# Wider streams and zero-padded rows in the small products of a decoder's mixers

## The chip, the cores and the metric

The kernel runs on one core of a Trainium2 chip. The metric is the device time of one execution in microseconds. Each kernel is run several times; the median counts. The kernel before took 3079.33 us (median of three runs, 3071.02 to 3081.82).

## What is computed

A decoder trunk of two layers over 512 tokens, with 16 learned meta tokens put ahead of them and dropped at the end; the width is 1024. Cut to what matters:

```python
h = concatenate([meta, x])                                   # 528 x 1024
for l in range(2):
    h = layer_norm(ALPHA * h + 0.5 * swiglu(h, ffn1...))     # width 2816
    h = layer_norm(ALPHA * h + mixer(h, ...))
    h = layer_norm(ALPHA * h + 0.5 * swiglu(h, ffn2...))
return h[16:]

def mixer(x):
    z = x @ w_in                       # convolution branch, RWKV branch, two gates
    yc = conv_branch(glu_a, glu_b)     # 31 taps per channel, norm, product
    yr = rwkv_branch(zr)               # per head of 64, step by step over the tokens:
                                       #   S = S * w_t + (S @ -kk_t) (kk_t a_t)^T + v_t k_t^T
                                       #   y_t = S @ r_t
    return (sigmoid(gate_c) * yc + sigmoid(gate_r) * yr) @ w_out
```

In the RWKV branch `kk` is divided by its norm over the 64 columns of its head. All values are float32.

## The kernel before

Activations lie with the channels on the 128 partitions and the tokens along the row. A wide product of float32 values is made of three products of a split format: each operand is split into a high and a low part, and high*high, high*low and low*high are added up in PSUM. The weights stream through all the time: load from HBM on SP's queue, high part on ScalarE, low part on VectorE or by an adding transfer that GpSimd issues.

A layer is FFN, mixer, FFN. In the trace the two mixers with their input projections lie at about 400 to 1040 and 1935 to 2565 us. In a mixer the 16 heads are worked in four groups of four, `q` = 0 to 3, each with two pairs of heads (two heads fill 128 partitions). For each group:

- `prep` projects r, k and v (products of L246), and scales them. The norms of `kk` come from L1144: the squares (128 channels by 128 tokens as weights) are multiplied by every fourth column of a block matrix of ones, 32 columns, of which two are read: one of each head. Five such products make a pair's norms; each shows as two instructions in the trace, as all plain float32 products do (the split ones show as one).
- `scores` multiplies within each chunk of 64 tokens (L1250 transposes, L1259), and within the 16 meta tokens (L1236). The scores of the meta tokens, the keys, the values and some results lie in the tile `small`, 16 partitions by 2048.
- `substitution` (VectorE) inverts 16 by 16 blocks; `inverse` joins them to inverses of 64 by 64: one product of 64 columns (L1333), then three rounds of `x = dt + vt^T x` (L1340). The first round makes all 64 columns; the second and third only the columns 32 to 63, as the first 32 are right after one round.
- `meta` works off the meta tokens before the scan begins: scores times values (L1365), the small inverse times that (L1371), then the state that the scan starts from and, in the first layer, the meta tokens' own output (both by the helper `pairs`, L1459). All contract over the 16 meta tokens, so they use 16 of the 128 rows of the array.
- `scan` walks over the eight chunks: state product (L1415), a copy on ScalarE, two sets of four products (L1428 and L1431), a copy on ScalarE, products with the scores (L1436), and the new state `sv` on VectorE, which the next chunk's L1415 waits for.

Between these stand the projections of the next group, of the convolution's input and of the gates, all products of L246, as fill. VectorE also does the convolution's taps (L1088). The program is written as an interleaving of generators with tables of numbers, and a scheduler, which has prices of its own for each instruction, then sets the order of each engine's queue by priorities. Each engine works its queue in order. Some idle places are filled with products whose results are never read (`keep`, L227).

Of the kernel before, what the change touches and what calls it, by code (L numbers as in the profile page):

```python
# [7 lines left out]
F32 = mybir.dt.float32  # L8
# [8 lines left out]
P = 128  # L17
# [3 lines left out]
NM = 16  # L21
# [8 lines left out]
HS = 64  # L30
# [68 lines left out]
class Trunk:  # L99
# [868 lines left out]
    def mixer_begin(self, zs, filler):  # L968

        nc, mp, d = self.nc, self.mp, self.d
        z = self.tmp()
        self.token_mix(zs[0], 24, z)
        nc.scalar.activation(z[0:64, :], z[0:64, :], AF.Tanh)
        x = self.tmp("kp", 1, F32R), self.tmp("k2", 1, F32R)
        self.split(z, *x)
        z = self.tmp()
        self.token_mix(zs[1], 25, z)
        nc.scalar.activation(z, z, AF.Tanh, scale=0.5)  # L980
        xg = self.tmp("a", 1, F32R), self.tmp("pinv", 1, F32R)
        nc.scalar.activation(xg[0], z, AF.Copy, bias=1.0)
        nc.vector.scalar_tensor_tensor(xg[1], z, 1.0, xg[0].bitcast(F32), op0=ALU.add,
                                       op1=ALU.subtract)
        filler(START[0])
        acts = (lambda o: (AF.Sigmoid, self.v1("w0", o), 1.0),
                lambda o: (AF.Tanh, self.half[:, 0, o:o + 1], 0.5))
        up = [(d["w_up"], slice(0, 64)), (d["a_up"], slice(64, P))]

        room = mp.tile([P, 4, KT, P], F32R, name="sb", bufs=1)  # L990
        w = self.wunit(*((r, u[self.l].rearrange("r (o c) -> r o c", c=P)) for u, r in up),
                       dst=[room[:, 0], room[:, 1]])

        self.bi = 0
        stage = {}

        def lowrank(w, x, o, r, dst, act=None):
            if act is None:
                t = self.tmp("v", 4) if o % 2 else mp.tile([P, NCH * 4, 32], F32, name="b4",
                                                           bufs=B4)  # L1000
                t = t if o % 2 else t.rearrange("p a b -> p (a b)")[:, 0:T]
            else:
                if o == 0:
                    stage[r.start] = self.rows().rearrange("p q e f t -> p (q e f) t")
                t = stage[r.start][:, o]
            both = self.sc() if self.bi % 2 == 0 else None
            self.bi += 1
            for h in range(2):
                s = slice(h * (T // 2), (h + 1) * (T // 2))
                pm = (self.sm(("tr", "ch")[h]) if both is None else both[:, h])[:, :T // 2]  # L1010
                for j, (a, b) in enumerate(((0, 0), (0, 1), (1, 0))):
                    nc.tensor.matmul(pm, w[a][r, o, :], x[b][r, s], start=j == 0, stop=j == 2)
                to = t[:, s]
                if both is not None:
                    if h == 0:
                        continue
                    pm, to = self.pv(both), self.tv(t)
                if act is None:
                    nc.vector.tensor_scalar_mul(to, pm, 0.5)
                else:  # L1020
                    f, b, scale = act(o)
                    nc.scalar.activation(to, pm, f, bias=b, scale=scale)
            nc.sync.dma_start(out=dst[o * P:(o + 1) * P, :], in_=t)

        wg = self.wunit(d["g_up"][self.l].rearrange("r (o c) -> r o c", c=P),
                        dst=[room[:, 2], room[:, 3]])
        todo = [[lambda o=o, r=r, act=act, dst=dst: lowrank(w, x, o, r, dst, act)
                 for o in range(KT)]
                for (_, r), act, dst in zip(up, acts, (self.ds, self.as_))]
        todo.append([lambda o=o: lowrank(wg, xg, o, slice(0, P), self.ggs) for o in range(KT)])  # L1030
        for i, (j, o) in enumerate(LOW):
            todo[j][o]()
            if i % LOWSTEP == LOWSTEP - 1:
                filler(1)
            self.taps(TAP0[0])
        filler(START[1])
        self.sb = mp.tile([P, NCH, 4, 2 * C], F32, name="sb", bufs=1)

        self.ut = mp.tile([P, NCH * 2, C], F32, name="ut")

        small = mp.tile([NM, 2048], F32, name="small")
        self.small, o = {}, 0
        for name, n in (("kb", 512), ("s", 256), ("v", 256), ("u", 256), ("y0", 256), ("y1", 256), ("y2", 256)):
            self.small[name] = small[:, o:o + n]
            o += n

        self.dd = mp.tile([P, NCH * 2, 2, C], F32, name="dd")
        nc.gpsimd.memset(self.dd, 0.0)
# [66 lines left out]
    def prep_pair(self, q, p, Q):  # L1115
        nc, mp = self.nc, self.mp
        pc = Q["pc"]
        i = 2 * q + p
        cs = slice(i * P, (i + 1) * P)
# [5 lines left out]
        nk, r = G[:, 1, 0, :], G[:, 1, 1, :]  # L1125
        kp = self.tmp("kp", 1)
        self.token_mix(self.proj(16 + 8 + i), 8 + i, kp)
        sq = self.tmp()
# [3 lines left out]
        a = self.tmp("a", 1)  # L1132
# [5 lines left out]

        pn = self.sc()
        pn, p0 = pn[:, 0], pn[:, 1]  # L1140
        tr = p0[:, NM:NM + 160]
        for j in range(5):
            k0 = NM + j * P if j < 4 else 0
            nc.tensor.matmul(tr[:, 32 * j:32 * j + 32], sq[:, k0:k0 + P], self.bones[:, ::4],  # L1144
                             start=True, stop=True)
        tr = tr[:, ::16]
        rs = mp.tile([P, 10], F32, name="rs", bufs=1)
        rx = self.tmp()[:, :4 * P].rearrange("p (j h v) -> p j h v", j=4, h=2)
        rx0 = mp.tile([P, P], F32, name="rx", bufs=1)[0:NM].rearrange("a (h v) -> a h v", h=2)
# [54 lines left out]
        for h in range(2):  # L1204
            nc.tensor.matmul(pn[:, h, :T // 2], rk, k2[:, h * (T // 2):(h + 1) * (T // 2)],
                             start=True, stop=True)
# [7 lines left out]
    def scores(self, q, Q):  # L1214


        nc, mp = self.nc, self.mp
        G, FB, SB = Q["G"], Q["FB"], self.sb
        tr = self.sm("tr")
        for p in range(2):  # L1220
# [1 line left out]
                nc.tensor.transpose(tr[0:NM, f * 256 + p * P:f * 256 + (p + 1) * P],  # L1222
                                    FB[p][:, f * NM:(f + 1) * NM], self.ident)
        kb0 = self.small["kb"]
        nc.scalar.copy(kb0, tr[0:NM, :])
        Q["kb0"] = kb0.rearrange("p (f h v) -> p f h v", f=2, h=4)
        ps = self.sc()
        ps = [ps[:, 0], ps[:, 1]]
        s0 = Q["s0"] = self.small["s"].rearrange(
            "a (e p f g t) -> a e p f g t", e=2, p=2, f=2, g=2)  # L1230
        for e in range(2):
            p0 = ps[e][0:NM, 0:4 * 2 * NM].rearrange("a (p f x) -> a p f x", p=2, f=2)
            r = slice(HS * e, HS * e + HS)
            for p in range(2):
                for f in range(2):
                    nc.tensor.matmul(p0[:, p, f, :], FB[p][r, f * NM:(f + 1) * NM],  # L1236
                                     G[r, p, 1, :, 0:NM], start=True, stop=True)
            nc.vector.tensor_tensor(s0[:, e].rearrange("a p f g t -> a (p f) g t"),
                                    ps[e][0:NM, 0:4 * 2 * NM]
                                    .rearrange("a (x g t) -> a x g t", g=2, t=NM),  # L1240
                                    self.msk0[:, None].to_broadcast([NM, 4, 2, NM]), op=ALU.mult)
            nc.sync.dma_start(out=self.ms0[q, e::2].rearrange("h j t -> j h t"),
                              in_=s0[:, e, :, 1, 0, :])
        yield
        for c in range(NCH):
            cs = slice(NM + c * C, NM + (c + 1) * C)
            fs = slice(2 * cs.start, 2 * cs.stop)
            ps = self.sc()
# [7 lines left out]
            for p in range(2):  # L1256
                for e in range(2):
                    r = slice(HS * e, HS * e + HS)
# [58 lines left out]
    def inverse(self, q, g, Q):  # L1317
# [3 lines left out]
        nc, mp = self.nc, self.mp  # L1321
# [13 lines left out]
        x = dt  # L1335
        for c0 in (0, 2 * NM, 2 * NM):
            cs = slice(c0, C)
            for i in range(N):
                for r in halves:
                    nc.tensor.matmul(ps[r, i, cs], vt[r, i], x[r, i, cs], start=True, stop=True)  # L1340
            nc.vector.tensor_tensor(y[:, :, cs], ps[:, :, cs], dt[:, :, cs], op=ALU.add)
            x = y
        out = Q["G"].rearrange("a p e f t -> a (p e) f t")
# [9 lines left out]
    def meta(self, q, Q):  # L1353
# [3 lines left out]
        tr = self.sm("tr")  # L1357
        for p in range(2):
            nc.tensor.transpose(tr[0:NM, p * P:(p + 1) * P], Q["v"][p][:, 0:NM], self.ident)
        v0 = hc(self.small["v"])  # L1360
        nc.scalar.copy(v0, hc(tr[0:NM, 0:256]))
        s0, kb0 = Q["s0"], Q["kb0"]
        ch = self.sm("ch")
        for h in range(4):
            nc.tensor.matmul(ch[0:NM, h * HS:(h + 1) * HS], s0[:, h % 2, h // 2, 0, 0, :],  # L1365
                             v0[:, h, :], start=True, stop=True)
        sa0 = hc(self.small["u"])
        nc.scalar.copy(sa0, hc(ch[0:NM, 0:256]))
        ch = self.sm("ch")
        for h in range(4):  # L1370
            nc.tensor.matmul(ch[0:NM, h * HS:(h + 1) * HS], xt0[:, h, :], sa0[:, h, :],  # L1371
                             start=True, stop=True)
        nc.scalar.copy(sa0, hc(ch[0:NM, 0:256]))
        ch = self.sm("ch")
        self.pairs([(ch[HS:P, h * HS:(h + 1) * HS], kb0[:, 0, h, :], v0[:, h, :],
                     kb0[:, 1, h, :], sa0[:, h, :]) for h in range(4)])
# [4 lines left out]
        if not self.last:  # L1381
            ch = self.sm("ch")
            self.pairs([(ch[0:NM, h * HS:(h + 1) * HS], s0[:, h % 2, h // 2, 0, 1, :], v0[:, h, :],
                         s0[:, h % 2, h // 2, 1, 1, :], sa0[:, h, :]) for h in range(4)])
            y0 = self.small[f"y{q % 3}"].rearrange("a (m h v) -> a m h v", m=1, h=4)
            nc.scalar.copy(y0[:, 0], hc(ch[0:NM, 0:256]))
            Q["y0"] = y0

    def scan(self, q, Q):

# [378 lines left out]
```

## Time and profile before

| | |
|---|---|
| median of three runs | 3079.33 us |
| profiled execution, its own time | 3072.55 us |
| its span from the first to the last instruction | 3070.8 us |
| TensorE busy | 2996.3 us |
| VectorE busy | 2276.7 us |
| ScalarE busy | 1439.3 us |
| GpSimd busy | 178.3 us |
| mean granted clock of TensorE | 0.982 |

TensorE's busy time counts a product from its start until its modelled end, so what one costs in a stream is read from the starts of neighbouring groups, not from its duration. The page's clock row gives, for 40 slices of the span, the share of TensorE's full clock that was granted; a table by stretches gives it for any stretch.

### The profile page before, as it was taken

The numbers are of one execution on the slowest core, as the hardware profiler recorded it, in microseconds if no ns is written. First come the engines' busy times: TensorE is split into PE (matmuls) and PEld (weight loads), VectorE is DVE, ScalarE is ACT, GpSimd is POOL, SyncE is SP. The second block draws the span as 40 slices with busy tenths as digits, with TensorE's granted clock in tenths as the row PEclk, the third lists the DMA queues.
The fourth block names the chain that finished last, engine by engine and source line by source line (L and its number), as shares of the span: only waits on it lengthen the run. The fifth ranks groups of instructions, "written<-read, shape, count | busy, mean of one in ns | idle before, by whom it ended". The sixth has DMA issues, their size and how long they took to land. (4 is left out here: it accounts for less than half of the span.)

```text
span 3070.8 us, 64144 instructions
## 1 busy us (share of the span) xinstructions
PE 2996.3 (98%) x26076; PEld 2875.1 (94%) x26076; DVE 2276.7 (74%) x4689; ACT 1439.3 (47%) x2553; POOL 178.3 (6%) x286
## 2 busy tenths in 40 slices
PE   9999999999999999999999999999999999999998
PEld 9999989889888899999999999998889889999998
DVE  5766777788876768676776768778988748677767
ACT  4544464344455535444444444543454545254443
POOL 0110000000000000000001100000000000001100
PEclk9999999899999999999999999999999989999999
DMA  7665444335465554565545654443354645556652
GB/s 197 145 145 130 117 141 144 88 82 130 106 148 139 164 150 124 133 154 124 128 128 141 142 136 112 153 134 97 86 141 105 150 118 175 148 124 148 151 139 62
DMA packets 556149, 405.29 MB, mean 132 GB/s; under 512 B 89306, under 2 KB 500798, under 8 KB 555854
## 3 DMA queue, kind: packets, MB, share of 16 engines
q1 hardware_dynamic: 520302, 308.49, 35.2%
q0 software_dynamic: 30944, 84.18, 14.9%
q10 hardware_dynamic: 4608, 8.52, 0.7%
q8 instruction: 205, 3.36, 0.5%
q14 instruction: 90, 0.74, 0.1%
HBM read 270.81 MB, written 47.12 MB: 104 GB/s over the span
## 5 line engine op out<-in xcount | busy, mean ns | idle before, releaser
L217 PE MATMUL mm<-xh,w_hi 128*128 128x264 f32 (+1 forms) x1792 | 510.3, 286 | 7.5 <-ACT xh L460 5.9
L217 PE MATMUL mm<-xl,w_hi 128*128 128x264 f32 (+1 forms) x1792 | 509.1, 284 | 0.7 <-DVE xl L461 0.3
L217 PE MATMUL mm<-xh,w_lo 128*128 128x264 f32 (+1 forms) x1792 | 507.7, 284 | 0.0
L217 PE MATMUL mm<-hh,w_hi 128*128 128x264 f32 (+1 forms) x1408 | 399.7, 284 | 2.6 <-ACT hh L112 2.6
L217 PE MATMUL mm<-hh,w_lo 128*128 128x264 f32 (+1 forms) x1408 | 399.8, 284 | 0.0
L217 PE MATMUL mm<-hl,w_hi 128*128 128x264 f32 (+1 forms) x1408 | 399.5, 284 | 0.2
L246 PE MATMUL mm<-xh,w_hi 128*128 128x264 f32 x1760 | 388.8, 298 | 7.2 <-DVE kp L962 3.8
L246 PE MATMUL mm<-xh,w_lo 128*128 128x264 f32 x1760 | 384.1, 296 | 6.5 <-DMA w_lo<-w_raw 6.1
L246 PE MATMUL mm<-xl,w_hi 128*128 128x264 f32 x1760 | 386.6, 296 | 0.0
L1088 DVE SCALAR_TENSOR_TENSOR cacc<-cu,cw,cacc 128x528 f32<-128x528 f32 (+1 forms) x480 | 355.6, 754 | 3.5
L217 PEld LDWEIGHTS mm<-xh,w_hi 128*128 128x128 f32 x1792 | 337.1, 189 | 11.4 <-ACT xh L460 8.5
L217 PEld LDWEIGHTS mm<-xl,w_hi 128*128 128x128 f32 x1792 | 339.0, 189 | 2.7 <-DVE xl L461 2.5
L217 PEld LDWEIGHTS mm<-xh,w_lo 128*128 128x128 f32 x1792 | 338.7, 189 | 0.0
L122 ACT CAST w_hi<-sums 128x512 fp32r<-128x512 f32 (+1 forms) x204 | 155.0, 760 | 314.6 <-PE mm L217 202.7
L246 PEld LDWEIGHTS mm<-xh,w_hi 128*128 128x128 f32 x1760 | 284.5, 194 | 15.2 <-DVE kp L962 4.3
L246 PEld LDWEIGHTS mm<-xh,w_lo 128*128 128x128 f32 x1760 | 283.1, 194 | 14.0 <-DMA w_lo<-w_raw 7.5
L246 PEld LDWEIGHTS mm<-xl,w_hi 128*128 128x128 f32 x1760 | 283.4, 193 | 6.0
L217 PEld LDWEIGHTS mm<-hh,w_hi 128*128 128x128 f32 x1408 | 264.8, 188 | 3.2 <-ACT hh L112 3.0
L217 PEld LDWEIGHTS mm<-hl,w_hi 128*128 128x128 f32 x1408 | 265.0, 188 | 0.9 <-DVE hl L113 0.8
L217 PEld LDWEIGHTS mm<-hh,w_lo 128*128 128x128 f32 x1408 | 265.5, 189 | 0.1
L160 DVE TENSOR_TENSOR w_lo<-w_raw,w_hi 128x1024 fp32r<-128x1024 f32 (+1 forms) x194 | 204.2, 1055 | 74.5 <-ACT w_hi L149 70.0
L149 ACT CAST w_hi<-w_raw 128x1024 fp32r<-128x1024 f32 x134 | 140.6, 1051 | 247.2 <-PE mm L246 81.2
(366 smaller groups left out, 6819.9 us busy)
## 6 DMA issues: line engine op xcount, KB each, us to landing
w_raw<-in_w_in_dram SPq DMA_DIRECT2D x116, 512.0 KB
w_lo<-w_raw POOLq DMA_DIRECT2D x100, 512.0 KB, 4.9
w_raw<-in_ffn_wg_dram SPq DMA_DIRECT2D x88, 512.0 KB
w_raw<-in_ffn_wu_dram SPq DMA_DIRECT2D x88, 512.0 KB
w_raw<-in_ffn_wd_dram SPq DMA_DIRECT2D x80, 512.0 KB
w_lo<-w_raw POOLq DMA_DIRECT2D x68, 256.0 KB, 3.4
w_raw<-in_rwkv_wo_dram SPq DMA_DIRECT2D x16, 512.0 KB
w_raw<-in_conv_wo_dram SPq DMA_DIRECT2D x16, 512.0 KB
```

The lines of the kernel that those rows point to most:

```text
L122: self.nc.scalar.copy(hi, x)
L149: copy = self.nc.scalar.copy(hi[:, :kt], raw[:, :kt])
L160: sub = self.nc.vector.tensor_tensor(lo[:, k], raw[:, k], hi[:, k].bitcast(F32), op=ALU.subtract)
L217: self.issued = self.nc.tensor.matmul(pm, a[:, k, :], b[:, xk + k, s], start=first and k == 0 and j == 0, stop=last and k == nk - 1 and j ...
L246: m = self.issued = nc.tensor.matmul(pm[:, h, :n], a[:, wk + k, :], b[:, xk + k, s:s + n], start=first and k == 0 and j == 0, stop=last an ...
L1088: tap = nc.vector.scalar_tensor_tensor(y, x, w, y, op0=ALU.mult, op1=ALU.add)
```

## The change

Three kinds of small products get more columns or more rows, with the same results.

- The norm sums multiply by every second column of the block matrix: 64 columns, of which still two are read (every 32nd).
- The second and third round of the inverse stream all 64 columns into PSUM. VectorE still adds and writes only the columns 32 to 63.
- `small` has 128 partitions and is cleared once in each mixer by GpSimd. Products that take both operands from it contract over 128 rows, of which those below the 16 are zero: L1365 and the two uses of `pairs` (L1459). The writes go to the first 16 partitions, as before. The product with the small inverse (L1371) keeps its 16 rows, as its weights are in another tile.

```diff
-        small = mp.tile([NM, 2048], F32, name="small")
+        small = mp.tile([P, 2048], F32, name="small")
+        nc.gpsimd.memset(small, 0.0)
...
-        tr = p0[:, NM:NM + 160]
+        tr = p0[:, NM:NM + 320]
         for j in range(5):
             k0 = NM + j * P if j < 4 else 0
-            nc.tensor.matmul(tr[:, 32 * j:32 * j + 32], sq[:, k0:k0 + P], self.bones[:, ::4],
+            nc.tensor.matmul(tr[:, 64 * j:64 * j + 64], sq[:, k0:k0 + P], self.bones[:, ::2],
                              start=True, stop=True)
-        tr = tr[:, ::16]
+        tr = tr[:, ::32]
...
-        nc.scalar.copy(kb0, tr[0:NM, :])
+        nc.scalar.copy(kb0[0:NM], tr[0:NM, :])
...
-                    nc.tensor.matmul(ps[r, i, cs], vt[r, i], x[r, i, cs], start=True, stop=True)
+                    nc.tensor.matmul(ps[r, i], vt[r, i], x[r, i], start=True, stop=True)
...
-        nc.scalar.copy(v0, hc(tr[0:NM, 0:256]))
+        nc.scalar.copy(v0[0:NM], hc(tr[0:NM, 0:256]))
...
-            nc.tensor.matmul(ch[0:NM, h * HS:(h + 1) * HS], xt0[:, h, :], sa0[:, h, :],
+            nc.tensor.matmul(ch[0:NM, h * HS:(h + 1) * HS], xt0[:, h, :], sa0[0:NM, h, :],
                              start=True, stop=True)
-        nc.scalar.copy(sa0, hc(ch[0:NM, 0:256]))
+        nc.scalar.copy(sa0[0:NM], hc(ch[0:NM, 0:256]))
```

The number of instructions stays the same but for the two clears on GpSimd. Their order does not: the scheduler prices the wider products otherwise, and inside both mixers the queues of TensorE, VectorE and ScalarE are ordered anew. Outside the mixers the orders are equal. Two places on TensorE follow, where the scan waits for its own state. In all rows L246 is a projection product, and after the change line numbers are one higher.

The first place is the scan of the first group in the first mixer, fourth to sixth chunk. Before, from one chunk's transposes to the next state product (L1436 are the products with the scores, L1259 scores of the next group):

```order
L1406 MATMUL tr<-ident,v 128x128 x2
L1259 MATMUL sc<-G,FB 128x128 x2
L1436 MATMUL ch<-va,sb 128x64 x4
L1259 MATMUL sc<-G,FB 128x128 x2
L1415 MATMUL tr<-sv,G 64x64 x4
L1250 MATMUL sc<-ident,FB 128x128 x2
```

With the change, the same stretch:

```order
L1407 MATMUL tr<-ident,v 128x128 x2
L1251 MATMUL sc<-ident,FB 128x128 x2
L1437 MATMUL ch<-va,sb 128x64 x4
L246 MATMUL mm<-xh,w_lo 128x264
L1260 MATMUL sc<-G,FB 128x128 x4
L246 MATMUL mm<-xh,w_lo 128x264
L246 MATMUL mm<-xh,w_hi 128x264 x2
L246 MATMUL mm<-xl,w_hi 128x264
L1416 MATMUL tr<-sv,G 64x64 x4
```

Five projection products and two more score products now stand between the products with the scores and the state product.

The second place is the last chunk of the last group in the second mixer. Before (L1538 are transposes of the output):

```order
L1538 MATMUL tr<-ident,b_28598 128x128 x2
L246 MATMUL mm<-xh,w_lo 128x264
L1436 MATMUL ch<-va,sb 128x64 x4
L1415 MATMUL tr<-sv,G 64x64 x4
L1428 MATMUL ch<-w_30168,G 64x64
```

With the change:

```order
L1437 MATMUL ch<-va,sb 128x64 x4
L246 MATMUL mm<-xh,w_hi 128x264
L246 MATMUL mm<-xl,w_hi 128x264 x2
L246 MATMUL mm<-xh,w_lo 128x264 x2
L246 MATMUL mm<-xh,w_hi 128x264 x2
L246 MATMUL mm<-xl,w_hi 128x264 x2
L246 MATMUL mm<-xh,w_lo 128x264 x2
L246 MATMUL mm<-xh,w_hi 128x264
L1416 MATMUL tr<-sv,G 64x64 x4
L246 MATMUL mm<-xh,w_hi 128x264
L246 MATMUL mm<-xl,w_hi 128x264 x2
```

Twelve projection products have moved from other places of the mixer to between the last two chunks, and more follow behind the state product.

More of the change, by code (lines that the diff above doesn't have):

```diff
@@ L1237, in scores @@
                                      G[r, p, 1, :, 0:NM], start=True, stop=True)
-            nc.vector.tensor_tensor(s0[:, e].rearrange("a p f g t -> a (p f) g t"),
+            nc.vector.tensor_tensor(s0[0:NM, e].rearrange("a p f g t -> a (p f) g t"),
                                     ps[e][0:NM, 0:4 * 2 * NM]
@@ L1242, in scores @@
             nc.sync.dma_start(out=self.ms0[q, e::2].rearrange("h j t -> j h t"),
-                              in_=s0[:, e, :, 1, 0, :])
+                              in_=s0[0:NM, e, :, 1, 0, :])
         yield
@@ L1367, in meta @@
         sa0 = hc(self.small["u"])
-        nc.scalar.copy(sa0, hc(ch[0:NM, 0:256]))
+        nc.scalar.copy(sa0[0:NM], hc(ch[0:NM, 0:256]))
         ch = self.sm("ch")
         for h in range(4):
-            nc.tensor.matmul(ch[0:NM, h * HS:(h + 1) * HS], xt0[:, h, :], sa0[:, h, :],
+            nc.tensor.matmul(ch[0:NM, h * HS:(h + 1) * HS], xt0[:, h, :], sa0[0:NM, h, :],
                              start=True, stop=True)
-        nc.scalar.copy(sa0, hc(ch[0:NM, 0:256]))
+        nc.scalar.copy(sa0[0:NM], hc(ch[0:NM, 0:256]))
         ch = self.sm("ch")
@@ L1385, in meta @@
             y0 = self.small[f"y{q % 3}"].rearrange("a (m h v) -> a m h v", m=1, h=4)
-            nc.scalar.copy(y0[:, 0], hc(ch[0:NM, 0:256]))
-            Q["y0"] = y0
+            nc.scalar.copy(y0[0:NM, 0], hc(ch[0:NM, 0:256]))
+            Q["y0"] = y0[0:NM]
     def scan(self, q, Q):
```

## The prediction

> **What bounds the kernel now.** I read the page's first part, then its clock row, then the two mixers' stretches, the clock by stages, and last the order of the products on TensorE around each stage.
>
> ```profile
> span 3070.8 us, 64144 instructions
> PE 2996.3 (98%) x26076; PEld 2875.1 (94%) x26076; DVE 2276.7 (74%) x4689; ACT 1439.3 (47%) x2553; POOL 178.3 (6%) x286
> PEclk9999999899999999999999999999999989999999
> 400.00:1040.00 640.00, 614.26 (x5903) 563.66 (x5903) 494.73 (x1196) 302.79 (x593) 24.86 (x61) 0.96 0.48 130
> 1935.00:2565.00 630.00, 607.27 (x5833) 559.10 (x5833) 481.76 (x1124) 297.72 (x582) 24.89 (x61) 0.96 0.49 131
> ```
>
> TensorE is the bound: 98% busy, and in the two mixers (400 to 1040 and 1935 to 2565 us) it idles 25.7 and 22.7 us only. But its granted clock there is 0.96, while it is 1.00 in nearly all of the FFNs. VectorE, with 77% in the mixers, is the next.
>
> The clock is never 0.96. It is 1.00 or 0.50, in blocks of 3.41 us on one fixed grid. These are the mixers' blocks at half clock, in the columns of a table by stretches (length, busy us of PE, PEld, DVE, ACT, POOL, clock, DMA):
>
> ```profile
> 581.13:591.37 10.24, 10.24 (x79) 9.74 (x78) 4.87 (x29) 3.19 (x6) 0.00 (x0) 0.50 0.06 20
> 826.89:837.13 10.24, 10.24 (x61) 9.98 (x58) 6.47 (x28) 3.38 (x7) 0.00 (x0) 0.50 0.18 53
> 2349.23:2356.06 6.83, 6.83 (x46) 6.77 (x43) 2.95 (x20) 2.09 (x4) 0.00 (x0) 0.50 0.04 12
> 2461.87:2472.11 10.24, 10.24 (x86) 9.35 (x84) 4.84 (x20) 4.03 (x9) 0.00 (x0) 0.50 0.15 55
> 601.61:608.43 6.82, 6.61 (x30) 6.31 (x30) 4.45 (x9) 1.63 (x5) 0.00 (x0) 0.50 0.37 59
> 652.81:666.46 13.65, 12.45 (x71) 10.38 (x72) 8.65 (x18) 3.44 (x10) 0.00 (x0) 0.50 0.19 49
> 2134.19:2141.02 6.83, 6.83 (x33) 6.83 (x33) 5.49 (x12) 0.00 (x0) 0.00 (x0) 0.50 0.19 17
> 2519.90:2526.72 6.82, 5.58 (x38) 4.64 (x39) 2.15 (x5) 1.21 (x4) 0.00 (x0) 0.50 0.42 134
> 929.29:936.11 6.82, 5.75 (x47) 4.99 (x46) 2.49 (x4) 1.06 (x1) 0.85 (x1) 0.50 0.69 131
> 2557.44:2560.86 3.42, 2.93 (x11) 2.75 (x12) 2.86 (x5) 1.65 (x2) 0.00 (x0) 0.50 0.55 158
> ```
>
> I sort them in three. **Group A**, the first four rows: 37.55 us, each after an inverse with the meta products in it; TensorE is busy all through. **Group B**, the next four: 34.12 us, after a wait in the scan or in the norm sums' stage. **Group C**, the last two rows and four between them: 27.30 us, after a wait for a weight transfer, for ScalarE or for a layer norm's sums.
>
> Why does the clock fall in group A, where TensorE never stands still? Here is the program of TensorE just ahead of the first block and in it (start, us, line, rows*columns of the weights, moving operand, count):
>
> ```profile
> 576.41 1.14 PE L1340 MATMUL sc<-dd,b 64*64 64x64 f32 x30
> 577.48 0.61 PE L1371 MATMUL ch<-small,xt 16*16 16x64 f32 x8
> 578.02 0.51 PE L246 MATMUL mm<-xh,w_hi 128*128 128x264 f32 x2
> 578.37 0.41 PE L246 MATMUL mm<-xl,w_hi 128*128 128x264 f32 x2
> 578.71 1.12 PE L1340 MATMUL sc<-b 64*64 64x32 f32 x32
> 579.76 1.14 PE L1459 MATMUL ch<-small 16*64 16x64 f32 x16
> 580.83 0.58 PE L246 MATMUL mm<-xh,w_lo 128*128 128x264 f32 x2
> 581.78 1.92 PE L1340 MATMUL sc<-b 64*64 64x32 f32 x32
> 583.63 1.88 PE L1459 MATMUL ch<-small 16*16 16x64 f32 x16
> 585.44 2.34 PE L1144 MATMUL sc<-bones,tmp 128*128 128x32 f32 x10
> L246 PE MATMUL mm<-xh,w_hi 128*128 128x264 f32 x1760 | 388.8, 298 | 7.2 <-DVE kp L962 3.8
> L1205 PE MATMUL sc<-k,rk 128*128 128x264 f32 x64 | 17.8, 402 | 0.0
> ```
>
> The last two rows give an estimate of a pass: the same 264 columns take 402 ns as plain f32 and 298 ns as the split format, so a second pass costs 104 ns, 0.39 ns per column and pass. Take as **weighted streaming** of a product its columns times its passes (two in plain f32, one in the split) times 0.39 ns, times the share of the 128 rows that it uses. A projection product of L246 has 104 ns. One of 64 rows by 32 columns (L1340) has 12.6 ns, though 32 of them take 1.05 us, 33 ns each. One of 16 rows by 64 columns (L1459) has 6.3 ns of its 67 ns.
>
> The window from 577.71 to 581.13, the last before the clock falls, then holds 4 of L1371 (25 ns), four of L246 (416), 32 of L1340 (403), 16 of L1459 (101) and at most 200 ns of the next L246: 1.15 of 3.41 us, a share of about 0.33. I formed this share for all 900 windows of the span (transposes as plain f32). Of the windows at full clock, the fifteen after which it halves (the opening and closing one left out) have 0.06 to 0.34; the lowest after which it stays full has 0.36. So the trace puts a threshold near 0.35 on rows times columns, and idle time is only one way below it.
>
> **The change, part by part.**
>
> *The padding and the clock.* The later inverse stages go to 64 columns (25.2 ns each), the meta products of L1365 and L1459 to 128 rows (50.4 ns). In that window: 25 + 416 + 806 + 806 + 200 ns, a share of 0.66. The windows ahead of the other three blocks of group A go from 0.30, 0.34 and 0.33 to 0.74, 0.74 and 0.61 in the same way. All four lie well above the threshold, so I take group A as gone. Its price: 32 products of L1340 take 1.85 us at half clock (581.78 to 583.63) and 1.05 at full (578.71 to 579.76), a ratio of 1.76; L246 has 1.8. 37.55 us x (1 - 1/1.8) = **-16.7 us**. Bounds: 0 if the threshold is not this, -16.7. Nothing else takes this gain at once, since VectorE waits for TensorE there (2.80 us before it can read the norm sums):
>
> ```profile
> 587.82 0.17 DVE L1150 TENSOR_SCALAR rs<-sc 128x10 f32<-128x10 f32 x1 [2.80 <-PE sc L1144]
> 642.07 1.00 PE L1436 MATMUL ch<-va,sb 128*128 128x64 f32 x8
> 643.00 0.71 PE L1259 MATMUL sc<-G,FB 64*128 64x128 f32 x8
> 666.82 0.68 PE L1415 MATMUL tr<-sv,G 128*64 128x64 f32 x8
> 667.43 0.39 PE L246 MATMUL mm<-xh,w_lo 128*128 128x264 f32 x1
> 2253.91 1.26 PE L1144 MATMUL sc<-bones,tmp 128*128 128x32 f32 x10
> 2255.00 0.37 PE L246 MATMUL mm<-xl,w_hi 128*128 128x264 f32 x1
> L1048 POOL MEMSET dd<- 128x2048 f32 x2 | 3.6, 1808 | 0.0
> ```
>
> *What the padding costs on TensorE, at full clock.* Inverse: 30 products of 64 columns take 1.07 us (576.41 to 577.48), 35.7 ns against 32.8 ns: 2.9 ns x 1024 = 3.0 us. Norm sums: ten of 32 columns take 1.09 us, 109 ns each; the nearest with 128 by 128 weights and 64 columns, L1436, take 0.93 us for eight, 116 ns: 7 ns x 160 = 1.1 us (up to 3 us by the slowest L1436 of the scan). Meta: 16 rows take 67 ns; the nearest with 128 rows and 64 columns, L1415, 0.61 us for eight, 76 ns: 9 ns x 256 products = 2.3 us. Together +6.4, taken as **+7 us** (bounds +3, if narrow and wide cost alike in the inverse, and +9).
>
> [...]
>
> *The zeros.* One more clear of 128 by 2048 on GpSimd per mixer, which costs 1.81 us like that of `dd`; GpSimd is 6% busy and the first copy into `small` comes over 100 us later: **0** (1.8 us of GpSimd's queue, 3.6 if it were ever waited for).
>
> *The order.* No other instruction is added, but TensorE's, VectorE's and ScalarE's orders in both mixers change, as the two places above show. Some scan steps of the before order stand almost bare: state product (L1415), transposes, scan products, score products, and no projection in between. There TensorE waits for VectorE's state update:
>
> ```profile
> 650.53 0.65 PE L1415 MATMUL tr<-sv,G 128*64 128x64 f32 x8 [1.47 <-DVE sv L1443]
> 657.26 1.09 PE L1415 MATMUL tr<-sv,G 128*64 128x64 f32 x8 [1.20 <-DVE sv L1443]
> 2520.22 1.08 PE L1415 MATMUL tr<-sv,G 128*64 128x64 f32 x8 [1.57 <-DVE sv L1443]
> 601.40 0.66 PE L246 MATMUL mm<-xh,w_hi 128*128 128x264 f32 x2 [2.90 <-DVE kp L962]
> ```
>
> In the new order projection products stand between most of these steps (five of them, 0.6 us, ahead of one state product where none stood, twelve, 1.5 us, at the end of the second mixer). They fill the wait and raise the share of the window. Of group B, 652.81, 2134.19 and 2519.90 (27.30 us at half clock) lie at such places. If all go: 27.30 x 0.44, less a fifth for the waits inside them, -9.6 us, and some 4 us of waits. I take half of it, since a new order brings new late operands that no row shows: **-6 us** (bounds -14, and +15 if it opens five waits like that at 601.40).
>
> *Sum.* -16.7 + 7 - 6 = -15.7 us. The profiled execution took 3072.55 us, 6.8 under the median of 3079.33 of three others (3071.02 to 3081.82; mean of all four 3076.2). From the mean: **3060 us**. Group C stays.
>
> **Rivals.**
>
> *The order gives nothing back.* Group A goes, the padding costs 9 us, the new order's gains and losses cancel: -8, 3068 us. For it: half of group B hangs on how VectorE's queue now stands, which the order of TensorE does not tell. Chance 0.24.
>
> *The order cures more than that.* All of 27.30 us, the 6.82 us at 601.61 and its wait of 2.90: -16.7 + 6 - 14 - 6 = -31, 3046 us. For it: VectorE is freed in the former group A (4.87 of 10.24 us busy, held by TensorE), which comes just ahead of 601.40. Chance 0.14.
>
> *The clock goes by busy time.* The padding earns nothing and costs 7: 3083 us. Against it: group A. Chance 0.07.
>
> *Slower: late VectorE results at the projections.* Each wait like that of 601.40 costs 2.90 us and, by its window, 6.83 us at half clock, 3.0 us more: 5.9 us. In the order before, one of the sixteen norm stages has it at that length. With three such new ones the net -10 of padding and clock is nearly gone, from five on the kernel is over 0.5% slower: -10 + 5 x 5.9 = +20, 3096 us. For it: VectorE's rows move too, and it is 77% busy. Against: between the norm sums of neighbouring heads there stand more projections now than before. Chance 0.07.
>
> **How the numbers follow.** The forecast has 0.48. A measurement here tells 0.5% (15.4 us) from no change, so against the median faster means under 3064. The forecast's own scatter of 12 us around 3060 lies mostly below that: 0.40 of its 0.48, and with the cure 0.54 faster. The rest 0.08, with 0.24 and 0.07, is 0.39 same; slower 0.07. The range takes the costs' bounds and the first two rivals: 3041 to 3079.
>
> **What would show it.** Right: no block of 0.50 after an inverse with meta products; 64-column products of the inverse at 36 ns, norm sums at 116 ns, meta at 76 ns; mixers' mean clock up from 0.96 to about 0.98; fewer waits for `sv`. Wrong: blocks at the same places with the padding there (the threshold is another quantity), spacing of norm sums well over 129 ns (columns aren't covered by the weight load), or new waits over 2 us for VectorE in the mixers.

## The result and the profile after

The changed kernel takes 3046.45 us (median of six runs, 3041.0 to 3054.53) against 3076.49 us before (six runs on the same chip, 3071.02 to 3081.82). The ratio is 0.990, with a 95% interval of 0.988 to 0.992: about 30 us less, 1% faster. The forecast was 3060 us, within 3041 to 3079.

The page of the changed kernel, its span, TensorE's line and the clock row:

```profile
span 3046.1 us, 64152 instructions
PE 2971.7 (98%) x26076; PEld 2850.4 (94%) x26076; DVE 2279.3 (75%) x4689; ACT 1437.3 (47%) x2553; POOL 181.7 (6%) x288
PEclk9999999999999999999999999999999999999999
```

Subtract TensorE's busy time from the span: 74.4 us of idle time, and 74.5 us before (3070.8 - 2996.3). TensorE runs 26076 instructions in both. So, between these two executions, not a microsecond came from less waiting. TensorE was busy 24.6 us less with the same work, and the span is 24.7 us shorter. The two mixers' rows by stretches (length, busy us of PE, PEld, DVE, ACT, POOL, clock, DMA) say where: their clock went from 0.96 to 0.99.

```profile
400.00:1040.00 640.00, 617.03 (x6020) 565.90 (x6020) 510.70 (x1218) 309.17 (x607) 26.55 (x62) 0.99 0.49 132
1935.00:2545.00 610.00, 586.75 (x5762) 538.52 (x5761) 480.06 (x1113) 289.87 (x569) 21.71 (x49) 0.99 0.51 136
```

And here is TensorE's program at the place where the first block of group A stood (start, us, line, rows*columns of the weights, moving operand, count; changed lines are one further down than before), with the row of the stretch below:

```profile
579.64 0.28 PE L246 MATMUL mm<-xh,w_lo 128*128 128x264 f32 x1
579.85 1.15 PE L1341 MATMUL sc<-b 64*64 64x64 f32 x32
580.93 1.15 PE L1460 MATMUL ch<-small 128*64 128x64 f32 x16
582.01 0.39 PE L246 MATMUL mm<-xh,w_lo 128*128 128x264 f32 x1
...
582.69 1.15 PE L1341 MATMUL sc<-b 64*64 64x64 f32 x32
583.77 1.07 PE L1460 MATMUL ch<-small 128*16 128x64 f32 x16
...
585.60 1.22 PE L1145 MATMUL sc<-bones,tmp 128*128 128x64 f32 x10
586.63 0.37 PE L246 MATMUL mm<-xl,w_hi 128*128 128x264 f32 x1
```

```profile
579.85:587.00 7.15, 7.15 (x120) 6.70 (x120) 5.89 (x22) 3.16 (x5) 0.00 (x0) 1.00 0.58 162
```

The clock is 1.00 throughout. Read the starts: 32 instructions of the inverse with 64 columns take 1.08 us (579.85 to 580.93), where 32 with 32 columns took 1.05 us at full clock before. The ten norm sums take 1.03 us (585.60 to 586.63).

Half clock in the mixers fell from 98.97 us to 34.15. The blocks that are left:

```profile
598.15:601.57 3.42, 3.42 (x16) 3.20 (x15) 3.42 (x7) 0.64 (x1) 0.00 (x0) 0.50 0.36 103
628.87:632.29 3.42, 2.90 (x50) 2.82 (x52) 3.02 (x5) 1.45 (x3) 0.00 (x0) 0.50 0.56 187
919.00:925.83 6.83, 6.83 (x84) 6.10 (x82) 2.21 (x4) 0.36 (x1) 0.00 (x0) 0.50 0.58 156
1021.40:1024.82 3.42, 3.42 (x18) 3.42 (x17) 3.09 (x5) 2.35 (x4) 0.00 (x0) 0.50 0.29 79
2041.99:2045.40 3.41, 3.41 (x16) 3.20 (x15) 2.11 (x5) 1.56 (x2) 0.00 (x0) 0.50 0.12 37
2144.39:2147.80 3.41, 3.41 (x54) 3.24 (x53) 3.10 (x6) 0.80 (x3) 0.00 (x0) 0.50 0.49 151
2431.11:2437.94 6.83, 6.31 (x49) 5.86 (x50) 2.68 (x4) 0.61 (x1) 0.00 (x0) 0.50 0.31 52
2533.51:2536.92 3.41, 2.84 (x11) 2.66 (x12) 2.85 (x5) 1.55 (x2) 0.00 (x0) 0.50 0.49 137
```

Each of these follows a wait of TensorE of 1.7 to 4.8 us in or across the window ahead; three of them are in these rows, which end with the idle time before the instruction and who ended it:

```profile
597.69 0.72 PE L1157 MATMUL sc<-ident,tmp 128*128 128x128 f32 x4 [2.19 <-ACT tmp L1155]
2431.63 0.44 PE L1334 MATMUL sc<-dd,ut 64*64 64x64 f32 x2 [2.86 <-DMA dd<-xdscr]
2534.08 1.22 PE L415 MATMUL st<-ssum,ones 128*128 128x256 f32 x2 [4.78 <-DVE ssum L469]
```

No block is left of the kind in which TensorE never stood still. The waits themselves did not go. The view of waits (who waits for whom, us in total, times, longest) before:

```profile
PE tr L1415 <- DVE sv L1443: 8.2, 10, 1.6
PE mm L246 <- DVE kp L962: 3.8, 2, 2.9
PE sc L1156 <- ACT tmp L1154: 2.7, 2, 1.8
```

and after:

```profile
PE sc L1157 <- ACT tmp L1155: 7.6, 4, 2.2
PE tr L1416 <- DVE sv L1444: 7.3, 10, 1.7
```

VectorE's state update `sv` is waited for ten times in both. The wait of 2.9 us for `kp` is gone, and those for `tmp` in the norm stage have grown from 2.7 to 7.6 us.

### The profile page after: what moved, and what is told of

It reads as the page before. It is cut to its first block, busy times and chain, and to the rows that moved or that the text cites. A ratio compares the mean times of both kernels' runs of the same rounds, so it can differ in the third digit from the quotient of the medians.

```text
span 3046.1 us, 64152 instructions
## 1 busy us (share of the span) xinstructions
PE 2971.7 (98%) x26076; PEld 2850.4 (94%) x26076; DVE 2279.3 (75%) x4689; ACT 1437.3 (47%) x2553; POOL 181.7 (6%) x288
## 4 chain that ended last, share of the span: by engine, by line
PE 83%; DVE 7%; DMA 4%; ACT 3%; issue 2%; SPq 0%; ACTq 0%; DVEq 0%; POOLq 0%
PE mm L217 54%; PE mm L246 17%; PE sc L1341 2%; PE ch L1437 2%; PE tr L1416 1%; PE sc L1260 1%; PE ch L1429 1%; DVE cacc L1089 1%; DMA w_lo<-w_raw 1%; DVE ln_rstd L444 1%; PE sc L1012 1%; DVE w_lo L160 1%; DMA gscr<-glus 1%; PE sc L1334 1%; DVE xl L461 1%
## 5 line engine op out<-in xcount | busy, mean ns | idle before, releaser
L246 PE MATMUL mm<-xh,w_hi 128*128 128x264 f32 x1760 | 381.3, 293 | 3.7 <-DVE tmp L962 2.3
L246 PE MATMUL mm<-xh,w_lo 128*128 128x264 f32 x1760 | 379.4, 293 | 5.4 <-DMA w_lo<-w_raw 5.3
L246 PE MATMUL mm<-xl,w_hi 128*128 128x264 f32 x1760 | 381.5, 292 | 0.0
L217 PEld LDWEIGHTS mm<-xh,w_hi 128*128 128x128 f32 x1792 | 337.1, 189 | 11.4 <-ACT xh L460 8.5
L217 PEld LDWEIGHTS mm<-xh,w_lo 128*128 128x128 f32 x1792 | 338.6, 189 | 0.0
L246 PEld LDWEIGHTS mm<-xh,w_lo 128*128 128x128 f32 x1760 | 276.9, 190 | 13.4 <-DMA w_lo<-w_raw 6.5
L246 PEld LDWEIGHTS mm<-xh,w_hi 128*128 128x128 f32 x1760 | 278.0, 190 | 12.2 <-DVE tmp L962 2.8
L246 PEld LDWEIGHTS mm<-xl,w_hi 128*128 128x128 f32 x1760 | 278.3, 189 | 5.4
L160 DVE TENSOR_TENSOR w_lo<-w_raw,w_hi 128x1024 fp32r<-128x1024 f32 (+1 forms) x194 | 204.3, 1055 | 72.3 <-ACT w_hi L149 70.4
```

What stands on the lines that cost most here:

```text
L160: sub = self.nc.vector.tensor_tensor(lo[:, k], raw[:, k], hi[:, k].bitcast(F32), op=ALU.subtract)
L217: self.issued = self.nc.tensor.matmul(pm, a[:, k, :], b[:, xk + k, s], start=first and k == 0 and j == 0, stop=last and k == nk - 1 and j ...
L246: m = self.issued = nc.tensor.matmul(pm[:, h, :n], a[:, wk + k, :], b[:, xk + k, s:s + n], start=first and k == 0 and j == 0, stop=last an ...
```

## The experiments

Two things were open after the result. Is the cause of group A really the weighted streaming, or the new order of instructions, or busy time? And which of the three parts brought what? The scheduler prices an instruction by its columns, so widening the norm sums or the inverse moves instructions, while adding rows to the meta products moves none. The kernel before and its copy with the meta's zeros therefore have one order on every engine; so have the two kernels with only the norm sums widened, the two with only the inverse widened, and the two with both. Each pair shows the meta's zeros alone, at a fixed order.

### The meta's zeros alone, in the order of before

```
-        small = mp.tile([NM, 2048], F32, name="small")
+        small = mp.tile([P, 2048], F32, name="small")
+        nc.gpsimd.memset(small, 0.0)
 ...     (all meta operands `small` over 128 rows; inverse and norm sums as before)
```

> The kernel before with one part alone: the zeros under the 16 rows of the meta's small tiles, and the meta products over 128 rows. The inverse and the norm sums are as before, and every engine's instructions stand in the order of before, so nothing but the streamed rows differs. Theory A (the clock of a 3.41-us block goes by the columns streamed, weighted by the rows that carry them, in the block ahead; threshold about 0.36): in the four blocks ahead of group A the share goes from 0.32-0.36 to 0.52-0.58, so the half-clock blocks at 581, 827, 2349 and 2462 us go and those of groups B and C stay: 37.55 us of half clock less, 14 to 17 us faster, ratio 0.9945 to 0.9955, about 3061 us. Theory B (the gain of the change came from its other order): no gain, 0.999 to 1.001, all of group A still there. Theory C (the clock goes by busy time): as B, with up to 2 us of padding on top.

Measured: 3063.08 us (12 runs), ratio 0.996, interval 0.9947 to 0.9974, about 12 us less, a little under the 14 to 17 us expected. All four blocks of group A are gone. This is the place of the first (its timeline, then the row of that stretch):

```profile
580.49 1.12 PE L1341 MATMUL sc<-b 64*64 64x32 f32 x32
581.54 1.15 PE L1460 MATMUL ch<-small 128*64 128x64 f32 x16
583.29 1.12 PE L1341 MATMUL sc<-b 64*64 64x32 f32 x32
584.35 1.07 PE L1460 MATMUL ch<-small 128*16 128x64 f32 x16
585.34 1.31 PE L1145 MATMUL sc<-bones,tmp 128*128 128x32 f32 x10
```

```profile
580.49:591.28 10.79, 10.79 (x150) 10.40 (x150) 7.55 (x39) 3.87 (x6) 0.00 (x0) 1.00 0.31 87
```

The inverse is as narrow as before, the order is the same, TensorE is as busy as before, and the clock is 1.00 instead of 0.50. What differs is that 112 rows of zeros are streamed along. So in these two runs neither order nor busy time makes group A; the rows do: with 16 of them the stretch ran at 0.50, with 128 at 1.00. The other blocks stayed, as expected, but not quite: at 647.9 us one was 17.07 us long (13.65 before), and a new one of 6.83 us came at 852.7 (elsewhere one of 3.41 us went and another grew by as much), so the mixers' half clock went to 71.7 us and not to 61.4.

### The change without the meta's zeros

```
 ...     (inverse over 64 columns, norm sums over 64 columns)
-        nc.gpsimd.memset(small, 0.0)
+        small = mp.tile([NM, 2048], F32, name="small")
```

> The change without the zeros and the 128-row meta products: the inverse over all 64 columns and the norm sums over 64, in the order of the changed kernel on every engine. Theory A: with the inverse's columns alone the blocks after inverse and meta keep a share of 0.42 or more, above the threshold, so no block of group A comes back and the time is that of the changed kernel within 3 us, 3043 to 3050 us, ratio 0.989 to 0.992. A variant of A in which the rows of the meta are what cures: 3 or 4 blocks of group A back, 3058 to 3064 us. Theory B (order): as the changed kernel, 3046 us; together with the run of the meta alone it tells B from A.

Measured: 3052.5 us (6 runs), ratio 0.9918, 0.9893 to 0.9944; the upper end expected was 3050 us. Every block that is left follows a wait, none a busy inverse: with the inverse's columns alone group A's half clock is gone too. But after a wait at 915 us, half clock lasted 17.07 us here and 6.83 us in the changed kernel, with the same instructions in the same order. In it stand these products (timeline), at half clock:

```profile
919.38 1.03 PE L1371 MATMUL ch<-small,xt 16*16 16x64 f32 x8
921.51 1.11 PE L1459 MATMUL ch<-small 16*64 16x64 f32 x8
922.55 1.97 PE L1340 MATMUL sc<-b 64*64 64x64 f32 x32
924.46 1.11 PE L1459 MATMUL ch<-small 16*64 16x64 f32 x8
929.02 1.88 PE L1459 MATMUL ch<-small 16*16 16x64 f32 x16
```

With the zeros the clock came back after two windows; without them it took five. The two parts are therefore two ways to the same cure, and what the zeros add to the inverse is smaller than what they bring alone.

### The clock by itself

A program of its own: 13 stretches of plain f32 products of one shape, none with a wait, and 64 wide products between two stretches.

```
+    part(200, 16, 64, 64, a)     # rows, columns of weights, columns streamed, operand
+    part(180, 128, 64, 64, a)
+    part(180, 128, 64, 64, zs)   # rows 16 to 127 are zeros
+    part(200, 64, 64, 32, a, halves)   # two halves of 64 rows, one after the other
+    part(200, 64, 64, 64, a, halves)
+    part(130, 128, 128, 32, a)   # then 40, 44, 48, 64 columns
 ...
+    part(200, 128, 16, 64, a)
+    part(200, 32, 64, 64, a)
+    part(200, 64, 64, 64, a)
```

> A program of its own that computes none of the reference: 13 stretches of 130 to 400 plain fp32 products of one shape, with no wait inside a stretch, with 64 products of 128x512 between them. Theory A (columns times rows/128, two passes each, 0.417 ns a column at the spacing seen; threshold 0.35 to 0.37 of a block): half clock in the stretches of 16 rows x 64 columns (share about 0.1), 32 rows x 64 (0.2), 128 rows x 32 columns (0.25) and x 40 (0.31); on the edge 128 rows x 44 and x 48, 64 rows x 64 one product at a time (0.34 to 0.38); full clock at 128 rows x 64 columns, with zeros in 112 of the rows as with none (0.49 to 0.66), at pairs of 64-row products of 64 columns in the two halves (0.75), and at 128 rows x 64 columns with 16 columns of weights (0.8). Theory C (busy time): all thirteen at full clock, since TensorE waits for nothing in any. A theory D, in which zeros do not count: the stretch with zeros at half clock like the one of 16 rows.

Measured in one profiled execution: rows of stretches inside the 13 parts, in their order (length, busy us of PE, clock, DMA):

```profile
40.00:72.00 32.00, 32.00 (x303) 0.50 0.01 2
95.00:110.00 15.00, 15.00 (x261) 1.00 0.01 2
130.00:146.00 16.00, 16.00 (x278) 1.00 0.01 2
165.00:184.00 19.00, 19.00 (x660) 1.00 0.02 4
203.00:222.00 19.00, 19.00 (x658) 1.00 0.02 4
245.00:290.00 45.00, 45.00 (x213) 0.50 0.00 0
320.00:356.00 36.00, 36.00 (x171) 0.50 0.00 0
385.00:424.00 39.00, 39.00 (x185) 0.50 0.00 0
452.00:492.00 40.00, 40.00 (x190) 0.50 0.00 1
514.00:538.00 24.00, 24.00 (x217) 1.00 0.00 1
557.00:575.00 18.00, 18.00 (x326) 1.00 0.01 3
605.00:626.00 21.00, 21.00 (x199) 0.50 0.01 2
650.00:668.00 18.00, 18.00 (x313) 1.00 0.01 2
```

TensorE is busy 100% in all thirteen by the profile, and six run at half clock. Half: 16 rows, 32 rows, and 128 rows with 32, 40, 44 or 48 columns. Full: 64 rows, 128 rows with 64 columns, with zeros as with data, and with 16 columns of weights as with 128. So in these thirteen rows the clock goes with rows times streamed columns in a given time. It does not go with the number of weight columns (1.00 with 16 as with 128), the values (1.00 with zeros as with data) or busy time (100% in the six at 0.50 as in the seven at 1.00; theory C had all thirteen at full clock).

By the prediction's measure, an estimate: an instruction with 128x128 weights and 64 columns is 111 ns from the next at full clock (24 us by 217). In the kernel before, those with 32 columns (L1144) and with 64 (L1436) both stand 112 ns apart at full clock (medians), so those with 48 are taken at 111 too. With 48 columns that is 48 x 2 x 0.39 / 111 = 0.34 and it falls; with 64 columns 0.45 and it stays. The two passes of plain f32 are also an estimate: in the kernel before, instructions of 264 columns stand 222 ns apart as plain f32 (L1205) and 122 ns as the split format (L246), at full clock. Full-clock instructions of 64 rows and 64 columns (18 us by 313, 57.5 ns) have 25 / 57.5 = 0.43 and stay. The value that parted the mixers' windows before, near 0.35, lies inside. On the edge my expectation erred once: 64 rows one at a time stay clearly above the threshold. For halves with 32 columns it gave no clock; they have 12.5 ns of 28.8, or 0.43, and stay too.

### Each part alone, and the change without it

The norm sums alone, and with the meta's zeros (the change without the inverse's columns):

```
-            nc.tensor.matmul(tr[:, 32 * j:32 * j + 32], sq[:, k0:k0 + P], self.bones[:, ::4],
+            nc.tensor.matmul(tr[:, 64 * j:64 * j + 64], sq[:, k0:k0 + P], self.bones[:, ::2],
```

> The kernel before with the norm sums alone over 64 columns; it brings an order of its own, since the scheduler sees ten products that cost more. Theory A (blocks after inverse and meta fall to half clock because of their thin streaming): those four blocks (group A, 37.55 us) stay, since neither inverse nor meta is touched; their gain of 15 us is not there. What else it gives is the order or the wider sums at the waits of scan and norm stage (group B, 34.12 us of half clock): if these carry group B's recovery in the changed kernel, B falls to some 10 us and the time to 3062-3066 us; if not, 3073-3079 us.

> The change without the inverse's extra columns: norm sums over 64 columns and meta over 128 rows, in the order of the run of the norm sums alone on every engine. Theory A: the meta's rows alone lift the blocks of group A above the threshold, as they did in the order of before (half clock 98.97 to 72 us), so 13 to 16 us under the run of the norm sums alone; with group B cured by the norm sums or their order 3046 to 3051 us, otherwise 3060 to 3064 us.

The inverse alone, and with the meta's zeros (the change without the wider norm sums):

```
-                    nc.tensor.matmul(ps[r, i, cs], vt[r, i], x[r, i, cs], start=True, stop=True)
+                    nc.tensor.matmul(ps[r, i], vt[r, i], x[r, i], start=True, stop=True)
```

> The kernel before with the inverse alone over all 64 columns, with an order of its own. Theory A: group A gone by the columns alone (15 to 17 us), less 1 us of padding. If this order (not that of the norm sums) also carries group B's recovery: 3046 to 3052 us; if group B stays: 3059 to 3063 us. If group A were cured by the rows of the meta only, group A stays, 3073 to 3079 us.

> The change without the wider norm sums: inverse over 64 columns and meta over 128 rows, in the order of the run of the inverse alone on every engine. Theory A: group A gone; since the inverse's columns lift the blocks above the threshold by themselves, the meta's rows add little: the time of the run of the inverse alone within 3 us. If the norm sums are what cures group B, 3058 to 3063 us; if not, 3046 to 3050 us.

Measured, with the earlier runs, by order of instructions. Half clock is the sum of the mixers' blocks at 0.50 in the profiled execution, idle its span less TensorE's busy time from its page; the gain is (1 - ratio) x 3076 us.

| order | kernel | ratio, 95% | half clock, us | idle, us | gain, us |
|---|---|---|---|---|---|
| of before | before | 1 | 99.0 | 74.5 | 0 |
| of before | meta alone | 0.9960 (0.9947 to 0.9974) | 71.7 | 76.4 | 12 |
| with norm sums | norm sums alone | 0.9974 (0.9955 to 0.9993) | 92.2 | 71.9 | 8 |
| with norm sums | all but inverse | 0.9932 (0.9912 to 0.9952) | 61.4 | 70.8 | 21 |
| with inverse | inverse alone | 0.9940 (0.9919 to 0.9961) | 51.2 | 72.3 | 18 |
| with inverse | all but norm sums | 0.9924 (0.9907 to 0.9941) | 47.8 | 74.2 | 23 |
| with both | all but meta | 0.9918 (0.9893 to 0.9944) | 47.8 | 73.2 | 25 |
| with both | the change | 0.9904 (0.9884 to 0.9924) | 34.1 | 74.4 | 30 |

Read it in pairs. The meta's zeros bring 12 and 13 us where the inverse is narrow, and 5 and 4 us where it is wide (these two are within the uncertainty of some 6 us): meta and inverse overlap, as theory A has it. The inverse brings 18 us to the kernel before and 9 us on top of the other two. The norm sums bring 6 to 9 us each time they are added, whatever else is there, but each time the order changes with them, and each of these alone is near its uncertainty. No subset has a lower ratio than the whole change.

Idle time is 71 to 76 us in all eight, while half clock goes from 99 to 34: the gains are gains of clock. By the factor of 1.8 (in the kernel before, L246's products stand 220 ns apart at half clock and 122 ns at full) the block sums give 65 x 0.44 = 29 us for the whole change, against 24.7 us between the two profiled spans and 30 us between medians.

With the norm sums alone, blocks after a busy inverse stay, as theory A expects (at 582, 828, 954 and 2118 us). Nor does a wide inverse end half clock at a busy TensorE everywhere. With the inverse alone, one block of 3.41 us at 821 us follows an inverse with narrow meta products; with all but the norm sums, one of 6.83 us at 2398 us follows scan and score products of 64 rows. Neither has a wait ahead of it. Where expectations missed: the run of the norm sums alone did not cure group B either (92.2 us of half clock; blocks of 20.5 us at 630 and 10.2 us at 705 came where others went), yet was 8 us faster, of which its profile shows 3.7; the inverse's run landed where I had put "group B stays" (3058.49 us, expected 3059 to 3063) though only 51 us of half clock were left; all but the inverse (3055.36 us) and all but the norm sums (3054.47 us) landed between the two times given for each. The runs with a wide inverse are 2 to 5 us slower between profiles than their blocks say (inverse alone: 16.6 us shorter, where 48 us less half clock in the mixers, and 2.5 us more outside, give 20). The spacing of the inverse accounts for less than 1 us of that. What the rest is stayed open.

### Feeding the two longest waits

```
+FEED = (11, 18)
         mean = st()
+        if head:
+            self.keep(mean, head)
-        nc.tensor.matmul(mean[:, :n], self.ones, ssum[:, s], start=True, stop=True)
+        m = nc.tensor.matmul(mean[:, :n], self.ones, ssum[:, s], start=True, stop=True)
```

> The changed kernel with 11 and 18 products of ones, 128x512 (some 0.225 us each), ahead of the first layer norm's mean product at the two ends of the mixers, into a tile that the mean product then overwrites: the waits of 3.06 us (before 1020.7) and 4.78 us (before 2534.1) for VectorE's sum are filled with streaming. Theory A: the half-clock blocks at 1021.4 and 2533.5 us go, 2 x 3.41 / 2 = 3.4 us less, and the waits stay in length: 3043 us, 0.998 to 1.000 of the changed kernel. If the products delay the mean product: no gain or up to 2 us worse, with the blocks gone all the same. Theory C (busy time): blocks gone too, so this run does not tell A from C; it tells whether waits of 3 to 5 us are what halves the clock in what is left.

Measured: 3049.36 us, ratio 0.9918 (0.9893 to 0.9943): no gain over the changed kernel's 3046.45 us, and 2.9 us more is within the spread of either. The rows of the two waits show why:

```profile
1023.94 0.71 PE L418 MATMUL st<-ssum,ones 128*128 128x264 f32 x2 [2.61 <-DVE ssum L475]
2534.83 1.22 PE L418 MATMUL st<-ssum,ones 128*128 128x256 f32 x2 [4.08 <-DVE ssum L475]
```

They are still there, and so are the blocks behind them (1024.8 and 2533.5 us). I had put the products ahead of the wrong layer norm: these two waits are those of the convolution's norm, and the products went to the norm after the output projection, which has the same line. There they stand in TensorE's way: 29 products of some 0.225 us are 6.5 us. From the place where each set goes in to the next `keep` products behind it, which both kernels have, this run takes 2.8 and 4.0 us longer than the changed kernel, all at full clock. So the run says nothing on its question, and one thing besides: here the filler products, where there was no wait, cost their full time. It also shows how far blocks wander at a fixed order: up to that point the program is the changed kernel's, and yet the block at 598 is gone, one of 3.41 us is at 844, and that at 919 lasts 10.2 us instead of 6.8. Single blocks of one execution should not be read too finely.

## Why the prediction was right, and where it was wrong

**The bound and the measure: right.** TensorE set the time before and after, idle time did not change, and the weighted streaming decided the clock. The runs of the meta alone (1.00 and not 0.50 at the place of group A's first block, in the order of before) and of the clock by itself (six shapes at 0.50 with TensorE busy 100%) show it; the rival of busy time has fallen.

**Group A, -16.7 us: right in kind.** All four blocks are gone in the changed kernel, and in the copy with the meta's zeros alone. That copy gained 12 us rather than 16.7; in its profile 10.2 us of half clock had appeared at other places.

**The padding, +7 us: a term of the sum that was mis-sized.** It measured about +1. The inverse's 32 instructions went from 1.05 to 1.08 us (0.8 ns each, not 2.9; 0.8 us over 1024). The norm sums take 103.3 ns each with 32 and with 64 columns (median of stretches at full clock, not one single place), not 116. The sixteen meta instructions take 1.08 us (580.93 to 582.01), where 1.07 us stood before: 67 ns, not 76. The step that failed was to price by the nearest row of like shape: L1436 and L1415 have as many columns and rows as the padded products and yet take longer, so their extra nanoseconds do not come from columns or rows; what they come from stays open. The nearer row was the product itself.

**The order, -6 us: mis-sized too, and for a wrong reason in part.** Outside group A, half clock fell from 61.4 to 34.1 us, nearly all of it at group B's places (34.1 to 10.3 us); by the factor of 1.8 that is an estimate of 27.3 x 0.44 = -12 us. I had split the term into half clock and waits, and expected fewer waits for `sv`. There are as many (ten), and idle time is the same to 0.1 us. One of the three blocks that I put down to these waits had another cause: ahead of 2134.19 TensorE waited 1.15 us for ScalarE's copy (`va`, L1421). What went is not the waits but most of the half clock behind them: the two blocks left after a wait for `sv` (629 and 2144) last 3.4 us each. Right behind the state product in both stand not the projections that I had named but the first round of an inverse (L1341, 32 instructions of 64 columns, as wide before the change as after). Whether these end the blocks so soon was not tested. How much of these 12 us is the order and how much the wider columns stays open: the scheduler prices by columns, and a kernel with the one and not the other was not run.

**Group C stays: right.** Five of its six blocks have one at a like place after (919, 1021, 2042, 2431, 2534), 23.9 us of the 34.1 that are left.

**The sum.** With the padding as measured and the order as estimated from the blocks: -16.7 + 1 - 12 = -27.7 us, from 3076.2 to 3048.5 us. The time was 3046.45. The forecast of 3060 was 14 us too slow. It fell on the number of the rival in which the order cures more (3046 us), but not by that rival's account: the padding cost nearly nothing instead of 6 us, and a wait in the norm stage stayed, as one for `tmp`. That the number fits is in part luck. The slower rival's new waits at the projections did not come; the one such wait there was is gone. GpSimd's zeros cost nothing that shows: POOL is busy 3.4 us more (178.3 to 181.7) and no one waits.

## What to carry to other kernels

If a stage is full of small products and the granted clock there is below 1, add up rows times columns per window before looking for waits: here TensorE ran at 0.50 with 100% busy, in group A's four blocks and with six of the thirteen shapes, and at 1.00 where the products streamed more rows or columns. Padding narrow products with columns or rows of zeros that no one reads cost about 1 us of 3046 here, where the spacing hardly moved with it (33 and 34 ns in the inverse and 103 and 103 ns in the norm sums with 32 and 64 columns, 67 and 67 ns in the meta with 16 and 128 rows). Two paddings in one window did the work of one: the meta's zeros brought 12 and 13 us beside the narrow inverse, 5 and 4 us beside the wide one. To price a wider product, look at the product's own spacing first, and measure the same place at full clock several times, rather than at a neighbour of like shape.

## What the runs showed of the hardware

These are measurements of this case's own profiles, those of the eight kernels and of the program of single shapes; nothing beyond these shapes was tested.

- Rows of zeros counted for the clock like data: in the program of single shapes, 180 products of 128 rows by 64 columns ran at 1.00 with 112 rows of zeros as without, and 200 of 16 rows alone at 0.50. In the mixers the place of group A's first block ran at 0.50 with 16 rows and at 1.00 with 112 rows of zeros added, in the same order.
- The number of weight columns did not count: in the program of single shapes, 16 columns of weights with 64 streamed columns ran at 1.00, 128 columns of weights with 48 streamed at 0.50.
- One share parts the windows of 3.41 us in all eight kernels. At the prediction's estimate of 0.39 ns per column and pass, 83 of the 84 windows after which the clock halved, those of the opening and the end left out, had a share of at most 0.35 (one had 0.38); of the nearly 6800 windows that stayed at full clock two lay under 0.35. In the changed kernel the nine that were followed by half clock had 0.00 to 0.32, and the lowest that stayed 0.35.
- The same share told how long the clock stayed down. With a column at half clock counted twice as long (0.78 ns; L1205's instructions stand 440 ns apart at half clock and 222 at full), windows with a share of up to 0.74 were followed by another at half clock, and windows with 0.71 or more by full clock: in columns, some 0.36 to 0.37 of what full clock could stream, close to the share at which it fell. But at half clock busy narrow products stood about twice as far apart (in the kernel before 107 ns and not 58 with 16 rows by 64 columns, L1459, and 213 and not 112 with 128 by 64, L1436), so that a stage of them, once it had fallen, stayed down: 17.07 us without the meta's zeros, 6.83 us with them.
- In the mixers at full clock, 32 or 64 columns cost the same 103.3 ns with 128x128 weights (the norm sums, stretches of ten), and 16 or 128 rows the same 67 ns (the meta products of L1459, stretches of sixteen).
